# Five of eight pairs by seven products in the output projection, and the stream of weight sums at seven steps

## The chip, the core and the metric

The kernel runs on one core of a Trainium2 chip. The metric is the device time of one execution in microseconds, as the median of several runs. A core has a matrix engine (TensorE, PE in the profile, with PEld for its weight loads), a vector engine (VectorE, DVE), a scalar engine (ScalarE, ACT), GpSimd (POOL) and SyncE (SP), which here issues the loads. Each works through a queue of instructions of its own, in the order of that queue.

## The reference

One layer of a transformer block for 256 tokens and a model width of 2048, all in float32. Three attentions and a gate over them are followed by an output projection, and that by a feed-forward part with a causal convolution of three taps:

```python
merged = (g[:, :, 0] * (o_fox @ w_br_fox[l])
          + g[:, :, 1] * (o_sb @ w_br_sb[l])
          + g[:, :, 2] * (o_mem @ w_br_mem[l]))
x = x + merged @ w_out[l]                                  # 2048 x 2048

h2 = rms_norm(x, g_ffn[l])
u = causal_depthwise_conv(h2 @ w_up[l], conv_w[l], conv_b[l])   # 2048 x 11264
u_gate, u_val = jnp.split(u, 2, axis=-1)
x = x + (jax.nn.silu(u_gate) * u_val) @ w_down[l]          # 5632 x 2048
```

The change touches the last three matrix products.

## The kernel before

**Splits.** A float32 product is put together from rounded parts. Every piece of weights of 128 rows by 1024 columns is loaded into a `raw` buffer; ACT casts it to `hi` (L142 or L322) and DVE subtracts that from the raw piece to get `lo` (L143 or L323). `hi` and `lo` have four buffers each (`SBUFS`). The activations are split in the same way. In the output and down stages, a product of a weight block and an activation block is three matmuls (`three`, L328 to L330): `hi` with the high part, `hi` with the rest, and `lo` with the high part.

**Stages.** The queries, keys and values, the attentions and the gated branches come first. Then follow the output stage `o` (`w_out`, two blocks of 1024 output columns), the up stage `u` (`w_up`), and the down stage `d` (`w_down`, two blocks of 1024 columns, `nb` 0 and 1).

**Blocks.** `blocked` computes one such block. It walks over the pairs of 128-row tiles of the contraction (8 in `o`, 22 in `d`), and a plan string names what it does in turn. "e" is `eight`: the 2 x 2 block product of a pair by eight products, 24 matmuls. "s" is `seven`: the same by Strassen's seven products, 21 matmuls. For that, four sums T1 to T4 of the pair's weights are needed, and sums of its activations. "f" is `form`: the sums of the activations of the next pair, by `pair_sums` (8 instructions on DVE and some on ACT). Products that belong to several output blocks go to four extra banks Y, and `gather` adds these to the result `xres` on DVE behind the block's last seven, mixed with what follows it in the plan.

**Sums of weights.** For `o` and `d` the sums T1 to T4 are made in earlier stages, when DVE and the DMA queues have time: a pair of weight tiles is loaded into `pre_...`, `sums_in` makes the sums with three additions on DVE (L249 to L251), and the result is stored in DRAM as `kept_...`, from which `seven` reads them back. In the up stage the generator `pair_sums_ahead` does so, for all pairs of `d` that are left: it handles one pair in each `period` of steps, adds after `add` steps and stores after `store` steps. A step is one piece of the up stage. In the stages of the gates `seven_here` does without a store: it makes the sums with four additions of 512 columns in tiles of their own (`prepared`).

**Up stage.** 11 groups of 512 columns, `f0` from 0 to 40 in steps of four tiles, each in two halves (`s` 0 for the gate, 1 for the value). A half has 8 pieces; a piece is named by group, half and first tile, as in `lo_u_0_4` (the answers here leave out the group's number). Each piece has 8 matmuls of 512 columns with `hi` (L1231) and 8 of 256 with `lo` (L1232). Behind each half the convolution runs on ACT and DVE: `cr` (L1168), `u` (L1177), two filter steps `y` (L1183, L1184), the product `y` (L1190) and the split into `aT` (L177), on tiles of 256 columns.

**Order.** A scheduler of the framework sorts the instructions of each engine's queue, except those that are wrapped in `in_order` (`tc.keep_in_program_order`), which keep the order of the program among themselves. `later` puts a generator on a list of side work that `tick` advances by one step per piece.

Of the kernel before, what the change touches and what calls it, by code (L numbers as in the profile page):

```python
# [9 lines left out]
F32 = mybir.dt.float32  # L10
F32R = mybir.dt.float32r
# [31 lines left out]
def hybrid_block(  # L43
# [54 lines left out]
    def later(gen):  # L98
        waiting.append(gen)
# [24 lines left out]
    def finish():  # L124
        while waiting or active:
            tick(beside=False)
# [76 lines left out]
    def k_tiles(name):  # L203
# [19 lines left out]

    o_plans = ("eessesse", "eessesse")
    g_plans = (("", "esesesee", "esesesee"), ("esesesee", "esesesee", "esesesee"))
    d_plans = (
        "efefefef" + "sef" * 4 + "ssefsfssfssee",
        "efefef" + "sss" + "esss" * 3 + "ssee",  # L230
    )
    T1, T3, T4, T2 = range(4)
# [13 lines left out]

# [120 lines left out]
    def blocked(name, w, nb, n0, plan, pair, sums, raw_tile, t4_tile, gathered, ready=None, form=None, apart=None):  # L367
# [4 lines left out]
        ns = plan.count("s")  # L372

        def a_of(p, j, t):
            v = pair(p, j)
# [13 lines left out]
        def eight(p, first, last):  # L389
            by_bank = last and apart is not None  # L390
            w = []
            for j in range(2):
                w.append(parts(load(2 * p + j), f"{name}{nb}_{2 * p + j}"))
                if not by_bank:
                    for t in range(NT):
                        for n in range(2):
                            three(X[t][n], *a_of(p, j, t), w[j][n], first and j == 0, last and j == 1)
                go_on()
            if by_bank:
                for t in range(NT):  # L400
# [58 lines left out]
            three(Y[1], *f_of(p, FS2), T2w, first, last)  # L459
            go_on()  # L460

        by_seven = seven_here if name == "g" else seven
        ahead = {}
        s, e = 0, ns
        for i, c in enumerate(plan):
            if c == "s":
# [4 lines left out]
                by_seven(s, s == 0, s == ns - 1)  # L471
                s += 1
                if s == ns:
                    later(gathered(n0, Y))
            elif c == "f":
                form()
            else:
                eight(e, i == 0, i == len(plan) - 1)
                e += 1
            if name == "g" and plan[i + 1 : i + 2] == "s":  # L480
                ahead[s] = prepared(s)
        finish()
        return X

# [124 lines left out]
    def block(name, dt=F32):  # L609
        return bp.tile([P, 1024], dt, tag="blk", name=name)  # L610
# [384 lines left out]

    def merged_sums():
        yield 1
        for p in range(o_plans[0].count("s")):
# [119 lines left out]

    raw_o = lambda name: raw_tile(name, lambda name: gp.tile([P, PIECE], F32, tag="pre", bufs=1, name=name))
    t4_o = (junk, lambda name: block(name)[:, :512])  # L1120
    for nb, plan in enumerate(o_plans):
# [94 lines left out]
    for f0 in range(0, FT, 4):  # L1216
        if f0 == FA:
            assert not halves
            for g in background:
                deque(g, 0)  # L1220
            background.clear()
        for s in range(2):
            ps = [bank(f"u{f0 + i}_{s}") for i in range(4)]
            c0 = s * D_FF + f0 * P
            for k in range(0, KT, 2):
                hi, lo = piece(upv[:, k : k + 2, c0 : c0 + 512], 2, 512, f"u{f0}_{s}_{k}")
                for j in range(2):
                    first, last = k + j == 0, k + j == KT - 1
                    for i in range(4):
                        c = slice(i * P, (i + 1) * P)  # L1230
                        nc.tensor.matmul(ps[i], lhsT=hi[:, j, c], rhs=hT(k + j), start=first, stop=False)  # L1231
                        nc.tensor.matmul(  # L1232
                            ps[i][:, :S], lhsT=lo[:, j, c], rhs=hT(k + j)[:, :S], start=False, stop=last
                        )
# [16 lines left out]
        return dn[0].tile(shape, dt, tag=tag, name=name)  # L1251

    ov = out[0].rearrange("(t p) d -> p t d", p=P)
    N0, N1 = (plan.count("s") for plan in d_plans)
    sf = xt_pool.tile([P, 28, 2, P], F32R, tag="xt", name="sf")
    sf_more, sf_rest = [], []
    assert N0 == 11
# [3 lines left out]
    def s_of(p, f):  # L1261


        if f == FS1:
            return a_blocks[:, 2 * p, :, 1]
        if p < 9:
            return sf[:, 3 * p + f]
        if p == 9:
            return sf_more[0][:, f] if f < 2 else sf_rest[2]
        if p == 10:  # L1270
            return sf[:, 27] if f == 0 else sf_rest[f - 1]
        return a_blocks[:, 2 * (p - N0 + N1) + f // 2, :, f % 2]

    tmp_d = lambda name: place([P, PIECE], F32, "ts", name)

# [66 lines left out]
```

## Time and profile before

| | us |
|---|---|
| median of three runs | 1462.11 (1461.22 to 1462.31) |
| profiled execution | 1461.49 |
| its span on the core | 1459.8 |
| output stage, about | 658 to 743 |
| up stage, about | 743 to 1233 |
| down stage, first block, about | 1233 to 1345 |
| down stage, second block, about | 1345 to 1456 |

Times in the trace count from the start of the span. A row of the timeline gives the start, the duration, the engine, the line of the kernel, the operation, and what is written and read, with the number of equal instructions in a row; in brackets stands how long the engine was idle before it, and what released it. A row of the waits gives the waiting engine and its group, what released it, and then the sum, the number and the longest of those waits. In a table by windows the columns are busy times of PE, PEld, DVE, ACT and POOL, the granted clock, the share of the DMA engines and GB/s.

### The profile page before, as it was taken

To read this page: it belongs to the slowest core of one execution; us is meant where nothing else is said; L and a number is where in the kernel's file an instruction comes from. 1 tells how busy PE (TensorE), PEld (TensorE's weight loads), DVE (VectorE), ACT (ScalarE), POOL (GpSimd) and SP (SyncE) were. 2 spreads that over 40 slices of the span, in tenths; PEclk is the share of its full clock that TensorE was granted. 3 is DMA by queue.
4 is the path that set the end of the run, shared out by engine and by line. 5 is a ranking of instruction groups with operands and counts; after the bars stand their busy time and mean duration, and the time that the engine had idled before them with its cause. 6 is when DMAs were issued, how large, how long until landed. Compare 5 with 4: busy or idle time off the path is not lost.

```text
span 1459.8 us, 20547 instructions
## 1 busy us (share of the span) xinstructions
PE 1454.0 (100%) x7314; PEld 1230.1 (84%) x7314; DVE 1213.4 (83%) x1791; ACT 850.0 (58%) x1212; POOL 19.3 (1%) x48
## 2 busy tenths in 40 slices
PE   9999999999999999999999999999999999999998
PEld 7888888888888888888888888888888888888887
DVE  5778777776898899997887888888888877999878
ACT  6755454564564555545666556556556565676665
POOL 0000000010000000000000000000000000000000
PEclk9999999999999999999999999999999999999999
DMA  9697798777668576788877888888888866899995
GB/s 312 202 330 248 267 341 288 238 241 222 209 207 269 172 231 198 270 265 263 276 196 232 288 266 306 278 273 299 283 281 298 267 200 202 253 291 333 299 324 222
DMA packets 162534, 381.08 MB, mean 261 GB/s; under 512 B 12234, under 2 KB 27486, under 8 KB 158334
## 3 DMA queue, kind: packets, MB, share of 16 engines
q1 hardware_dynamic: 161022, 377.52, 78.9%
q10 hardware_dynamic: 1328, 2.11, 0.4%
q8 instruction: 57, 0.93, 0.3%
q14 instruction: 47, 0.39, 0.1%
q0 software_dynamic: 80, 0.13, 0.0%
HBM read 343.01 MB, written 36.70 MB: 260 GB/s over the span
## 4 chain that ended last, share of the span: by engine, by line
PE 97%; DVE 1%; DMA 1%; issue 0%; SPq 0%; ACT 0%; DVEq 0%; ACTq 0%
PE u L1231 22%; PE u L1232 11%; PE xd L329 3%; PE xd L330 3%; PE xd L328 3%; PE xg L330 3%; PE xg L329 3%; PE xg L328 3%; PE s L328 2%; PE s L330 2%; PE f L330 2%; PE f L328 2%; PE f L329 2%; PE s L329 2%; PE b L330 2%; PE b L328 2%
## 5 line engine op out<-in xcount | busy, mean ns | idle before, releaser
L1231 PE MATMUL u<-hT,hi_u 128*128 128x512 f32 x1232 | 428.3, 394 | 0.0
L1232 PE MATMUL u<-hT,lo_u 128*128 128x256 f32 x1232 | 341.3, 277 | 0.0
L1231 PEld LDWEIGHTS u<-hT,hi_u 128*128 128x128 f32 x1232 | 231.0, 188 | 53.8
L143 DVE TENSOR_TENSOR lo_u<-raw_u,hi_u 128x1024 fp32r<-128x1024 f32 x176 | 215.1, 1222 | 73.2 <-ACT hi_u L142 71.9
L142 ACT CAST hi_u<-raw_u 128x1024 fp32r<-128x1024 f32 x176 | 184.7, 1050 | 135.0 <-PE u L1231 106.7
L1232 PEld LDWEIGHTS u<-hT,lo_u 128*128 128x128 f32 x1232 | 231.2, 188 | 0.0
L323 DVE TENSOR_TENSOR lo_d<-raw_d,hi_d 128x1024 fp32r<-128x1024 f32 x88 | 106.7, 1222 | 16.2 <-ACT hi_d L322 13.8
L322 ACT CAST hi_d<-raw_d 128x1024 fp32r<-128x1024 f32 x88 | 91.7, 1053 | 38.8 <-PE xd L329 17.8
L322 ACT CAST hi_g<-raw_g 128x1024 fp32r<-128x1024 f32 (+1 forms) x80 | 77.1, 972 | 48.9 <-PE xg L329 19.2
L323 DVE TENSOR_TENSOR lo_g<-raw_g,hi_g 128x1024 fp32r<-128x1024 f32 (+1 forms) x80 | 88.6, 1119 | 4.1 <-ACT hi_g L322 4.1
L142 ACT CAST hi_f<-raw_f 128x1024 fp32r<-128x1024 f32 (+1 forms) x40 | 38.5, 967 | 51.8 <-PE f L329 42.8
L330 PE MATMUL xg<-lo_g,xT 128*128 128x512 f32 x175 | 68.1, 389 | 0.0
L329 PE MATMUL xg<-hi_g,xT 128*128 128x512 f32 x175 | 68.1, 389 | 0.0
L328 PE MATMUL xg<-hi_g,xT 128*128 128x512 f32 x175 | 68.1, 389 | 0.0
L143 DVE TENSOR_TENSOR lo_f<-raw_f,hi_f 128x1024 fp32r<-128x1024 f32 (+1 forms) x40 | 44.6, 1118 | 22.3 <-ACT hi_f L142 21.7
L143 DVE TENSOR_TENSOR lo_s<-raw_s,hi_s 128x1024 fp32r<-128x1024 f32 (+1 forms) x40 | 44.7, 1117 | 20.9 <-ACT hi_s L142 20.9
L1231 PE MATMUL u<-hT_rest,hi_u 128*128 128x512 f32 x176 | 62.0, 394 | 0.0
L142 ACT CAST hi_b<-raw_b 128x1024 fp32r<-128x1024 f32 x32 | 33.6, 1051 | 45.2 <-DMA raw_b<-in_w_br_fox_dram 15.8
L142 ACT CAST hi_s<-raw_s 128x1024 fp32r<-128x1024 f32 (+1 forms) x40 | 38.4, 961 | 36.8 <-PE s L329 23.9
L1182 ACT ACTIVATE y<-u,taps 128x256 f32<-128x256 f32 x88 | 49.6, 596 | 16.3 <-DVE u L1177 16.2
L330 PE MATMUL xd<-lo_d,aT 128*128 128x512 f32 x148 | 57.6, 389 | 0.0
L328 PE MATMUL xd<-hi_d,aT 128*128 128x512 f32 x148 | 57.6, 389 | 0.0
(520 smaller groups left out, 3473.1 us busy)
## 6 DMA issues: line engine op xcount, KB each, us to landing
raw_u<-in_w_up_dram SPq DMA_DIRECT2D x176, 512.0 KB, 4.5
raw_g<-in_w_in_dram SPq DMA_DIRECT2D x96, 512.0 KB, 4.4
raw_d<-in_w_down_dram SPq DMA_DIRECT2D x63, 512.0 KB, 5.4
pre_d<-in_w_down_dram SPq DMA_DIRECT2D x17, 1024.0 KB, 6.2
kept_d<-pre_d SPq DMA_DIRECT2D x17, 1024.0 KB, 6.2
raw_f<-in_w_in_dram SPq DMA_DIRECT2D x32, 512.0 KB, 4.9
raw_s<-in_w_in_dram SPq DMA_DIRECT2D x32, 512.0 KB, 5.2
raw_t_d<-kept_d SPq DMA_DIRECT2D x25, 512.0 KB, 5.8
```

What stands on the lines that cost most here:

```text
L142: pin(nc.scalar.copy(hi[:, :m], raw[:, :m]))
L143: pin(nc.vector.tensor_tensor(lo[:, :m], raw[:, :m], hi[:, :m].bitcast(F32), ALU.subtract))
L322: nc.scalar.copy(hi[:, :n], src)
L323: nc.vector.tensor_tensor(lo[:, :n], src, hi[:, :n].bitcast(F32), ALU.subtract)
L328: fix(nc.tensor.matmul(o, lhsT=ah, rhs=w[0], start=first, stop=False))
L329: fix(nc.tensor.matmul(o, lhsT=al, rhs=w[0], start=False, stop=False))
L330: fix(nc.tensor.matmul(o, lhsT=ah, rhs=w[1], start=False, stop=last))
L1182: nc.scalar.activation(y, u[:, 2:], AF.Identity, scale=tap(2), bias=tap(3))
L1231: nc.tensor.matmul(ps[i], lhsT=hi[:, j, c], rhs=hT(k + j), start=first, stop=False)
L1232: nc.tensor.matmul(ps[i][:, :S], lhsT=lo[:, j, c], rhs=hT(k + j)[:, :S], start=False, stop=last)
```

## The change

Each of the two output blocks does five of its eight pairs by seven, instead of three: pairs 0, 1, 2, 3 and 6 (`o_sevens`). The sums of the activations of pair 6 are made by a new generator `last_merged_sums` beside the first output block.

The stream of sums in the up stage makes one pair in 7 steps instead of 8, adds at once instead of after one step, and stores after 4 steps instead of 5. As the output stage takes four more pairs of those that are made early, this stream has 19 pairs to make instead of 17.

The second down block does 16 of its 22 pairs by seven instead of 14. For two of them, "i" in the plan, the sums are made on the spot: `begun` loads both tiles and makes three additions, and `seven_over` makes the fourth, both overwriting parts of the raw pieces. The plan's order is new: behind the last seven one "e" is left instead of two, and five "f" stand in it instead of three. The matmuls of the up stage are wrapped in `in_order`; they stand in the same order as before.

```diff
-    o_plans = ("eessesse", "eessesse")
+    o_plans = ("eessssse", "eessssse")
...
-        "efefef" + "sss" + "esss" * 3 + "ssee",
+        "efss" * 4 + "issefssisse",
...
+    o_sevens = (0, 1, 2, 3, 6)
+    pairs = lambda name, n: o_sevens if name == "o" else range(n)
...
-        for pr in range(plan.count("s"))
+        for pr, c in zip(pairs(name, 16), sevens(plan))
+        if c == "s"
...
+        def begun(p):
+            raw0, raw1, t13 = load(2 * p), load(2 * p + 1), tmp_d(f"t_{name}{nb}_{2 * p}")
+            b0, b1, u = (w.rearrange("p (n c) -> p n c", n=2) for w in (raw0, raw1, t13))
+            nc.vector.tensor_tensor(u[:, 0], b0[:, 0], b0[:, 1], ALU.add)
+            nc.vector.tensor_tensor(u[:, 1], b0[:, 1], b1[:, 1], ALU.add)
+            nc.vector.tensor_tensor(b0[:, 1], u[:, 0], b1[:, 1], ALU.add)
+            return raw0, raw1, t13
+
+        def seven_over(p, first, last):
+            raw0, raw1, t13 = ahead.pop(p)
+            (B00,) = parts(raw0[:, :512], f"{name}{nb}_{2 * p}")
+            three(Y[0], *a_of(p, 0, 0), B00, first, last)
+            nc.vector.tensor_tensor(raw0[:, :512], raw0[:, 512:], raw1[:, :512], ALU.add)
+            B10, B11 = parts(raw1, f"{name}{nb}_{2 * p + 1}")
...
+            T1w, T3w = parts(t13, f"t_{name}{nb}_{2 * p}")
...
+            T4w, T2w = parts(raw0, f"t_{name}{nb}_{2 * p + 1}")
...
+    def last_merged_sums():
+        yield 2
+        after = op.tile([P, KT, 2 * S], F32R, tag="ot", name="m_after")
+        ms[6] = after[:, 0:2].rearrange("p k c -> p (k c)").rearrange("p (f l q) -> p f l q", f=4, l=2)
+        pair_sums(mT[6], block("mw_6"), [(ms[6], slice(0, 4))])
...
-        pair_sums_ahead(lambda name: ends_tile(name, F32).rearrange("p i c -> p (i c)"), 8, 1, 5, delay=DU)
+        pair_sums_ahead(lambda name: ends_tile(name, F32).rearrange("p i c -> p (i c)"), 7, 0, 4, delay=DU)
...
-                        nc.tensor.matmul(ps[i], lhsT=hi[:, j, c], rhs=hT(k + j), start=first, stop=False)
...
+                        in_order(nc.tensor.matmul(ps[i], lhsT=hi[:, j, c], rhs=hT(k + j), start=first, stop=False))
```

DVE's queue in the up stage, group f0=12, first half, before the change, around the split of its third piece (`lo_u_0_4`):

```order
L251 TENSOR_TENSOR pre_d_0_8060<-pre_d_0_8060 128x512
L143 TENSOR_TENSOR lo_u_0_2_8137<-raw_u_0_2_8135,hi_u_0_2_8136 128x1024
L143 TENSOR_TENSOR lo_u_0_4_8181<-raw_u_0_4_8179,hi_u_0_4_8180 128x1024
L1168 TENSOR_TENSOR cr_1_8113<-cr_1_8113,u_1_7864 128x256
L1168 TENSOR_TENSOR cr_1_8124<-cr_1_8124,u_1_7865 128x256
L1177 TENSOR_TENSOR u_6990<-cr_1_8113,rbc 128x256
L1177 TENSOR_TENSOR u_6992<-cr_1_8124,rbc 128x256
L143 TENSOR_TENSOR lo_u_0_6_8203<-raw_u_0_6_8201,hi_u_0_6_8202 128x1024
L1183 TENSOR_SCALAR y_1_8117<-u_6990,taps,y_1_8117 128x256
L1183 TENSOR_SCALAR y_1_8128<-u_6992,taps,y_1_8128 128x256
```

The same place after the change (the lines of the code behind the new functions have larger numbers):

```order
L143 TENSOR_TENSOR lo_u_0_2_8166<-raw_u_0_2_8164,hi_u_0_2_8165 128x1024
L143 TENSOR_TENSOR lo_u_0_4_8210<-raw_u_0_4_8208,hi_u_0_4_8209 128x1024
L1208 TENSOR_TENSOR cr_1_8142<-cr_1_8142,u_1_7892 128x256
L1208 TENSOR_TENSOR cr_1_8153<-cr_1_8153,u_1_7893 128x256
L1217 TENSOR_TENSOR u_7018<-cr_1_8142,rbc 128x256
L1217 TENSOR_TENSOR u_7020<-cr_1_8153,rbc 128x256
L253 TENSOR_TENSOR pre_d_10_8231<-pre_d_10_8231 128x1024
L1223 TENSOR_SCALAR y_1_8146<-u_7018,taps,y_1_8146 128x256
L1223 TENSOR_SCALAR y_1_8157<-u_7020,taps,y_1_8157 128x256
L1224 TENSOR_SCALAR y_1_8146<-u_7018,taps,y_1_8146 128x256
```

and 15 rows further, the end of the same stretch:

```order
L1230 TENSOR_TENSOR y_0_7963<-y_0_7963,y_1_8190 128x256
L1230 TENSOR_TENSOR y_0_7972<-y_0_7972,y_1_8201 128x256
L255 TENSOR_TENSOR pre_d_10_8231<-pre_d_10_8231 128x512
L177 TENSOR_TENSOR aT<-y_0_7963,aT 128x256
L177 TENSOR_TENSOR aT<-y_0_7972,aT 128x256
L143 TENSOR_TENSOR lo_u_0_6_8238<-raw_u_0_6_8236,hi_u_0_6_8237 128x1024
L143 TENSOR_TENSOR lo_u_0_8_8260<-raw_u_0_8_8258,hi_u_0_8_8259 128x1024
```

Before, four instructions of the convolution stand between `lo_u_0_4` and `lo_u_0_6`, and the three additions of the stream's pair lie ahead, around the half's first pieces. After, 27 instructions stand there: 24 of the convolution and the three additions of `pre_d_10`.

DVE's queue at the program's end, before, from the addition of the second bank Y into `e`:

```order
L356 TENSOR_TENSOR e_13735<-e_13735,yd_1_12938 128x512
L323 TENSOR_TENSOR lo_d_42_13732<-raw_d_42_13729,hi_d_42_13731 128x1024
L323 TENSOR_TENSOR lo_d_43_13742<-raw_d_43_13739,hi_d_43_13741 128x1024
L358 TENSOR_TENSOR e_13735<-e_13735,yd_2_12939 128x512
L359 TENSOR_TENSOR xres_again<-xres_again,e_13735 128x512
L361 TENSOR_TENSOR e_13735<-e_13735,yd_3_12940 128x512
L362 TENSOR_TENSOR xres_again<-xres_again,e_13735 128x512
L364 TENSOR_TENSOR e_13735<-e_13735,yd_2_12939 128x512
L365 TENSOR_TENSOR xres_again<-xres_again,e_13735 128x512
L1303 TENSOR_TENSOR xres_again<-xres_again,xd_0_0_12786 128x512
```

After, from the last eight's first `lo`:

```order
L327 TENSOR_TENSOR lo_d_42_13820<-raw_d_42_13817,hi_d_42_13819 128x1024
L327 TENSOR_TENSOR lo_d_43_13826<-raw_d_43_13823,hi_d_43_13825 128x1024
L360 TENSOR_TENSOR e_13860<-e_13860,yd_1_12882 128x512
L362 TENSOR_TENSOR e_13860<-e_13860,yd_2_12883 128x512
L1346 TENSOR_TENSOR xres_again<-xres_again,xd_0_0_12828 128x512
L363 TENSOR_TENSOR xres_again<-xres_again,e_13860 128x512
L365 TENSOR_TENSOR e_13860<-e_13860,yd_3_12884 128x512
L1346 TENSOR_TENSOR xres_again<-xres_again,xd_0_1_12829 128x512
```

`lo_d_42` and `lo_d_43` are the pieces of the last eight. Before, all additions of `gather` stand ahead of those of that eight's banks (`xd`), and one eight more lies between them and the last bank Y; after, the two kinds alternate.

More of the change, by code (lines that the diff above doesn't have):

```diff
@@ L229, in hybrid_block @@
         "efefefef" + "sef" * 4 + "ssefsfssfssee",
-        "efefef" + "sss" + "esss" * 3 + "ssee",
+        "efss" * 4 + "issefssisse",
     )
+    sevens = lambda plan: [c for c in plan if c in "si"]
     T1, T3, T4, T2 = range(4)
@@ L371, in blocked @@
         Y = []
-        ns = plan.count("s")
+        ns = len(sevens(plan))
         def a_of(p, j, t):
@@ L460, in seven_here @@
             go_on()
-        by_seven = seven_here if name == "g" else seven
+        def begun(p):
[11 more added lines that the diff above has]
+            B10, B11 = parts(raw1, f"{name}{nb}_{2 * p + 1}")
+            three(X[0][0], *a_of(p, 1, 0), B10)
+            three(X[0][1], *f_of(p, FS4), B11)
+            go_on()
+            T1w, T3w = parts(t13, f"t_{name}{nb}_{2 * p}")
+            three(Y[2], *f_of(p, FS1), T1w, first, last)
+            three(Y[3], *f_of(p, FS3), T3w, first, last)
+            T4w, T2w = parts(raw0, f"t_{name}{nb}_{2 * p + 1}")
+            three(X[1][0], *a_of(p, 1, 1), T4w)
+            three(Y[1], *f_of(p, FS2), T2w, first, last)
+            go_on()
+        by_seven = {"s": seven_here if name == "g" else seven, "i": seven_over}
         ahead = {}
-        s, e = 0, ns
+        s, e = 0, 0
+        sp = pairs(name, ns)
+        ep = [p for p in range(len(plan) - plan.count("f")) if p not in sp]
         for i, c in enumerate(plan):
-            if c == "s":
+            if c in "si":
                 if s == 0:
@@ L477, in blocked @@
             else:
-                eight(e, i == 0, i == len(plan) - 1)
+                eight(ep[e], i == 0, i == len(plan) - 1)
                 e += 1
@@ L481, in blocked @@
                 ahead[s] = prepared(s)
+            elif plan[i + 1 : i + 2] == "i":
+                ahead[s] = begun(s)
         finish()
@@ L997, in merged_sums @@
         yield 1
-        for p in range(o_plans[0].count("s")):
+        for p in range(4):
             ms[p] = block(f"ms_{p}", F32R).rearrange("p (f l q) -> p f l q", f=4, l=2)
@@ L1120, in hybrid_block @@
     t4_o = (junk, lambda name: block(name)[:, :512])
+    later(last_merged_sums())
     for nb, plan in enumerate(o_plans):
@@ L1230, in hybrid_block @@
                         c = slice(i * P, (i + 1) * P)
-                        nc.tensor.matmul(ps[i], lhsT=hi[:, j, c], rhs=hT(k + j), start=first, stop=False)
-                        nc.tensor.matmul(
-                            ps[i][:, :S], lhsT=lo[:, j, c], rhs=hT(k + j)[:, :S], start=False, stop=last
+                        in_order(nc.tensor.matmul(ps[i], lhsT=hi[:, j, c], rhs=hT(k + j), start=first, stop=False))
+                        in_order(
+                            nc.tensor.matmul(
+                                ps[i][:, :S], lhsT=lo[:, j, c], rhs=hT(k + j)[:, :S], start=False, stop=last
+                            )
                         )
@@ L1253, in hybrid_block @@
     ov = out[0].rearrange("(t p) d -> p t d", p=P)
-    N0, N1 = (plan.count("s") for plan in d_plans)
+    N0, N1 = (len(sevens(plan)) for plan in d_plans)
     sf = xt_pool.tile([P, 28, 2, P], F32R, tag="xt", name="sf")
@@ L1271, in s_of @@
             return sf[:, 27] if f == 0 else sf_rest[f - 1]
-        return a_blocks[:, 2 * (p - N0 + N1) + f // 2, :, f % 2]
+        over = a_pair(p - N0 + N1).rearrange("p k (l t q) -> p k l t q", l=2, t=NT)
+        return over[:, f // 2, :, f % 2]
     tmp_d = lambda name: place([P, PIECE], F32, "ts", name)
```

2 lines of the change are left out of this document (1 added, 1 removed).

## The prediction

> **What bounds the kernel now.** I read the page's first two parts, then TensorE's waits, its steps in the timeline, and then the chain of work behind it in the up stage and in the last down block.
>
> ```profile
> span 1459.8 us, 20547 instructions
> PE 1454.0 (100%) x7314; PEld 1230.1 (84%) x7314; DVE 1213.4 (83%) x1791; ACT 850.0 (58%) x1212; POOL 19.3 (1%) x48
> PEclk9999999999999999999999999999999999999999
> PE spare L92 <- DVE qscale L531: 1.2, 1, 1.2
> PE kv L154 <- DVE memT L185: 0.5, 2, 0.2
> ```
>
> TensorE is busy for the whole span at its full granted clock, and the only waits of PE that the waits view lists are three at the very start, 1.7 us together. So the time is the count of matmuls times their step. Whatever another engine does is free until it makes TensorE wait once; from then on it counts in full. The change therefore has two sides: matmuls it removes, and waits it creates on an engine that has none.
>
> The step of a matmul is not its record, since they overlap:
>
> ```profile
> 1299.81 0.39 PE L328 MATMUL xd<-hi_t_d,aT 128*128 128x512 f32 x1
> ...
> 1311.83 0.39 PE L330 MATMUL yd<-lo_d,sf 128*128 128x512 f32 x1
> ```
>
> 53 steps of the down stage lie between these two starts, 12.02 us, so 0.227 us each.
>
> The work that feeds TensorE in the up stage is the split of every 128x1024 piece of weights into `hi` (a cast on ACT) and `lo` (a subtraction on DVE):
>
> ```profile
> L1231 PE MATMUL u<-hT,hi_u x1232: 389/395/474, 743.2 to 1230.0; 128*128 128x512 f32 x176
> L1232 PE MATMUL u<-hT_rest,lo_u x176: 274/277/280, 764.7 to 1233.0; 128*128 128x256 f32 x176
> ACT hi_u L142 <- PE u L1231: 106.7, 92, 1.9
> 917.07 1.05 ACT L142 CAST hi_u<-raw_u 128x1024 fp32r<-128x1024 f32 x1 [1.67 <-PE u L1231]
> 918.15 1.23 DVE L143 TENSOR_TENSOR lo_u<-raw_u,hi_u 128x1024 fp32r<-128x1024 f32 x1 [0.68 <-ACT hi_u L142]
> ```
>
> From 743.2 to 1233.0 are 490 us for 22 half groups of 8 pieces, 176 pieces: 2.78 us a piece. The casts waited 92 times, 106.7 us, for TensorE to give a `hi` buffer back: there are four, so the stock of split pieces is full most of the time, and it cannot be larger. How much time that stock is follows from the last two rows. TensorE ended a piece at about 917.07, and the buffer's next piece is wanted three pieces later, 917.07 + 3 x 2.78 = 925.4. Its `lo` is ready at 918.15 + 1.23 = 919.38. The lead is 6.0 us. It is the number on which this forecast turns: if DVE does other work W between two `lo_u`, the second one is ready W + 1.14 after the first, and is wanted 2.78 after it. So TensorE waits when W + 1.14 is over 6.0 + 2.78, that is W over **7.6 us**.
>
> Before, the trace has a drawdown of that kind without harm, at the stage's start:
>
> ```profile
> 768.43 1.23 DVE L143 TENSOR_TENSOR lo_u<-raw_u,hi_u 128x1024 fp32r<-128x1024 f32 x1 [0.53 <-ACT hi_u L142]
> 775.48 2.36 DVE L143 TENSOR_TENSOR lo_u<-raw_u,hi_u 128x1024 fp32r<-128x1024 f32 x2 [5.49 <-ACT hi_u L142]
> ```
>
> The two starts are 7.05 us apart, under the 8.8 us that the stock bears, and PE does not wait. There ACT and not DVE was late; it is the longest that the up stage shows.
>
> **Matmuls removed.** A pair by eight takes 24 matmuls and one by seven 21. Each o block turns one pair, the second down block two: 4 x 3 = 12 matmuls, 12 x 0.227 = **-2.7 us**. That is all that TensorE can win, and it is 0.19%. About 0.2%, 2.9 us, is what a measurement of this kernel tells from no change.
>
> **The o stage.** Two more sevens read stored sums, and the activations' sums of pair 6 are made beside the first block; DVE has free time there, and the streams that feed it come from earlier stages. I cost it at nothing. If the cover is gone, a late load costs up to a load's spare time, under 1 us each.
>
> **The up stage.** Its stream makes 19 pairs of sums instead of 17, one in 7 steps instead of 8. The price of two more is small in sum. What counts is where their three additions lie in DVE's queue:
>
> ```profile
> 923.70 1.23 DVE L143 TENSOR_TENSOR lo_u<-raw_u,hi_u 128x1024 fp32r<-128x1024 f32 x1 [0.16 <-ACT hi_u L142]
> 924.84 0.87 DVE L1183 SCALAR_TENSOR_TENSOR y<-u,taps,y 128x256 f32<-128x256 f32 x2
> 925.64 0.88 DVE L1184 SCALAR_TENSOR_TENSOR y<-u,taps,y 128x256 f32<-128x256 f32 x2
> 926.43 0.75 DVE L1190 TENSOR_TENSOR y<-y,y 128x256 f32<-128x256 f32 x2
> 927.10 0.41 DVE L1168 TENSOR_TENSOR cr<-cr,u 128x256 f32<-128x256 f32 x1
> 927.43 0.75 DVE L177 TENSOR_TENSOR aT<-y,aT 128x256 fp32r<-128x256 f32 x2
> 936.51 1.22 DVE L249 TENSOR_TENSOR pre_d<-pre_d 128x1024 f32<-128x1024 f32 x1
> 937.64 0.42 DVE L177 TENSOR_TENSOR aT<-y,aT 128x256 fp32r<-128x256 f32 x1
> 937.98 0.69 DVE L250 TENSOR_TENSOR pre_d<-pre_d 128x512 f32<-128x512 f32 x1
> 938.58 1.22 DVE L143 TENSOR_TENSOR lo_u<-raw_u,hi_u 128x1024 fp32r<-128x1024 f32 x1
> 939.71 0.69 DVE L251 TENSOR_TENSOR pre_d<-pre_d 128x512 f32<-128x512 f32 x1
> 940.38 1.23 DVE L143 TENSOR_TENSOR lo_u<-raw_u,hi_u 128x1024 fp32r<-128x1024 f32 x1
> ```
>
> From start to start: an addition of 256 columns 0.33 (927.10 to 927.43), a step of the filter 0.40 (two from 924.84 to 925.64), an addition of the stream 1.13 for the wide one and 0.60 and 0.67 for the others, a `lo` 1.14. Before, the stream's additions and the filter's stand between the `lo_u` in small lots. In the changed order the period of 7 walks through the 16 pieces of a group, and in four places the additions fall into one lot with the filter, with no `lo_u` between. The worst, shown with the change, is in group f0=12 from `lo_u_0_4` to `lo_u_0_6`: 16 additions of 256 columns, 8 filter steps, 3 additions of the stream, 5.3 + 3.2 + 2.4 = 10.9 us. Counted in the same way the other three lots are 8.9 (21 instructions, ending at a `lo_u_0_8`), 8.1 (19, `lo_u_1_6`) and 8.4 us (20, `lo_u_0_4`). Two more of 5.3 us follow a piece that is already late, and just pass.
>
> Over the 7.6 us that the stock bears, these are 3.3 + 1.3 + 0.5 + 0.8 = 5.9 us of waits of TensorE. With a lead 0.15 us larger, about what is left uncertain in reading it, 5.3. That is the lower end, since DVE cannot leave the order of its queue. The upper end counts whole records (0.42, 0.48, 1.22, 0.69) instead of starts: about 0.085 us more for each of these 87 instructions, 7.4 us, 13.3 together. The truth lies near the lower end, since the rows show the starts, but something comes on top: filter steps and `aT` lean on ACT, which does a 1.05 us cast between them, and in a lot they wait for it one after the other. I allow 0.4 us for each of the four, and take **+7.5 us** (5.3 to 13.3).
>
> [...]
>
> The matmuls of `u` (L1231, L1232) are now kept in program order; they stand in the same order before, so this costs nothing. The loads of the stream raise SyncE's traffic by two pairs in 490 us, which is hidden by the same stock.
>
> **The second down block.** Two pairs by seven have their sums made on the spot, and two more activation sums are formed within the block.
>
> ```profile
> 1344.00:1400.00 56.00, 56.00 (x248) 46.37 (x248) 47.45 (x64) 35.22 (x46) 0.00 (x0) 1.00 0.91 297
> 1400.00:1456.00 56.00, 55.83 (x252) 46.25 (x250) 46.34 (x49) 33.23 (x36) 0.00 (x0) 1.00 0.77 275
> L323 DVE TENSOR_TENSOR lo_d<-raw_d,hi_d 128x1024 fp32r<-128x1024 f32 x42 | 51.0, 1223 | 8.5 <-ACT hi_d L322 6.5
> L337 DVE TENSOR_TENSOR fw<-aT 128x512 f32<-128x512 f32 x3 | 2.1, 687 | 0.0
> L346 DVE TENSOR_TENSOR aT<-fw,aT 128x128 fp32r<-128x128 f32 x12 | 2.7, 286 | 0.0
> raw_d<-in_w_down_dram SPq DMA_DIRECT2D x23, 512.0 KB, 6.1
> ```
>
> DVE (fourth column of times) is busy 47.45 and 46.34 us in these 56 us each: 18.2 us are free. A pair on the spot needs 3.5 `lo`, 4.0 us, and four additions of 512 columns, 2.5 us, against two `lo`, 2.3 us: 4.2 more, 8.4 for both. A form is an addition of 0.7 us (L337), four of 0.22 (L346, 2.7 us for 12) and three small ones between them, about 2.5 us, two of them 5.0. So 13.4 of the 18.2 us are used up: in sum it just fits, with little to spare. The two raw pieces of such a pair are held until its last sums are split, so the loads behind them start late, and a load takes 6.1 us; I put that at 0 to 1 us.
>
> The end is worse placed. Of the two pairs by eight that stood behind the last seven one is left:
>
> ```profile
> 1443.81 0.39 PE L330 MATMUL yd<-lo_t_d,aT 128*128 128x512 f32 x1
> 1444.95 0.68 DVE L356 TENSOR_TENSOR e<-e,yd 128x512 f32<-128x512 f32 x1
> ...
> 1455.55 0.28 PE L330 MATMUL apart<-lo_d,a_ends 128*128 128x256 f32 x1
> 1455.95 0.42 DVE L1307 TENSOR_TENSOR xres_again<-xres_again,apart 128x256 f32<-128x256 f32 x1
> 1456.40 0.34 ACTq L1308 DMA_DIRECT2D out_dram<-xres_again  x1
> ```
>
> From TensorE's last matmul into Y1 to its last of all were 11.74 us. With one eight (24 x 0.227 = 5.4) less, 6.3 are left, and behind that Y1 and the last `lo` DVE still has 11 additions of 512 columns, at about 0.66 us 7.3 us, and one of 0.42. It ends 1.1 us later than TensorE lets it before. That is the floor; with the late loads and DVE's own backlog up to 4. I take **+2.5 us**.
>
> **Sum.** 1461.49 (the profiled execution) - 2.7 + 7.5 + 2.5 = 1468.8. The median of the runs is 0.62 above the profiled one: **1469.4 us**.
>
> **Rivals.**
> *The lots do no harm* (the lead is longer than I read, or ACT and DVE catch up): it decides at a lead of 9.3 us, five pieces and more. Against it stand the four buffers and the 92 waits for one of them. Then -2.7 + 1.1 to 4 at the end: 1460.5 to 1463.4, no measurable change. 0.14.
> *All is hidden*, the end too, and only the matmuls count: 1459.4; faster by over 0.2% only with the measurement's spread. 0.03.
> *The lots are stretched by ACT and the loads*: DVE's queue waits in each lot for a cast or an addition's 1 MB load, as at 775.48, where 5.49 us went. With 2 to 3 us for each of the four, 8 to 12 more than my 1.6: 1476 to 1480. 0.13.
> *TensorE slows down after waits.* The trace has one such stretch:
>
> ```profile
> 1.23 2.42 PE L92 MATMUL spare<-idle 128*128 128x384 bf16 x7 [1.23 <-DVE qscale L531]
> 6.39 0.39 PE L153 MATMUL kv<-hi_kv,memT 128*128 128x512 f32 x1
> 6.62 0.40 PE L154 MATMUL kv<-hi_kv,memT 128*128 128x512 f32 x1
> ```
>
> At the start seven matmuls of 384 columns take 2.42 us, 0.35 each, though by the later step of 0.23 for 512 they would take 0.17: half pace, for some 4 us, though the granted clock of the page shows 9 there too. If a wait of 3.3 us or more does that again, each costs about 2 us, one to three of them: 1471 to 1476. 0.12. [...]
>
> **Chances.** The forecast's own case (1466 to 1473) 0.58. The range that leaves out 2 in 10, part of the first rival and the far end of the third, is 1463.0 to 1478.5. Faster 0.03, same (1459.2 to 1465.0) 0.14, slower 0.83.
>
> **What would show it.** In the changed trace TensorE's waits should list `u` waiting for DVE's `lo_u`, four to six times, the longest about 3 to 4 us near the `lo_u_0_6` of f0=12, and the gaps before it filled with DVE rows and no `lo_u`. Behind the last matmul DVE should run for 1 to 3 us more. If the page shows PE without waits in the up stage, the lead is wrong and the first rival holds; if waits sit in the o stage or in the middle of the second down block, I have placed the price wrongly.

## The result, and the profile after

The changed kernel takes **1483.72 us** (median of five runs, 1478.64 to 1487.17) against 1461.61 (1461.22 to 1462.31): a ratio of **1.0147** (95% interval 1.0126 to 1.0168), 22 us slower. The forecast was 1469.4 with a range to 1478.5. The direction was right and the size was not. Two numbers of the text ahead of the prediction are wrong: before the change each output block did four of its eight pairs by seven, not three, and the two blocks together now take two more stored pairs, not four. This is why the stream makes 19 pairs instead of 17, and the prediction's 12 matmuls are counted rightly.

The page's head, of the profiled execution, which took 1487.17 us and is the slowest of the five:

```profile
span 1485.5 us, 20646 instructions
PE 1468.0 (99%) x7302; PEld 1235.7 (83%) x7302; DVE 1233.9 (83%) x1834; ACT 858.8 (58%) x1229; POOL 19.1 (1%) x48
```

TensorE has its 12 matmuls less, and is busy 14.0 us longer all the same. So a list of waits cannot hold the whole loss. Of the waits of PE:

```profile
PE u L1273 <- DVE lo_u L143: 7.5, 4, 4.4
PE yd L334 <- DVE lo_d L327: 2.0, 2, 1.2
...
PE hT L196 <- DVE xres_again L1169: 0.5, 1, 0.5
PE xd L334 <- DVE lo_d L327: 0.2, 1, 0.2
```

The four waits of `u` for `lo_u` are there, 7.5 us in all. What else became longer is seen when starts are compared. A half group has 8 pieces of 16 matmuls. From one start to the start 128 matmuls later, in the middle of the up stage, before:

```profile
999.84 0.40 PE L1231 MATMUL u<-hT,hi_u 128*128 128x512 f32 x1
...
1022.02 0.40 PE L1231 MATMUL u<-hT,hi_u 128*128 128x512 f32 x1
```

and after:

```profile
1004.66 0.40 PE L1271 MATMUL u<-hT,hi_u 128*128 128x512 f32 x1
...
1027.27 0.40 PE L1271 MATMUL u<-hT,hi_u 128*128 128x512 f32 x1
```

22.18 us before, 22.61 after: 2.77 and 2.83 us a piece, with nothing waited for between, and a granted clock of 1.00 in both. In the changed kernel's trace 172 of the 172 pieces counted (the first three are left out, and the few with a wait in them count by the pattern around them) run at 2.83; before, none does. That is about 0.053 x 172 = 9.1 us which no view of waits shows. The step is long from the first counted piece, at 755.0 us, and the first of the four waits comes 136 us later: in this execution the waits did not bring it about.

The longest wait, in DVE's timeline of after:

```profile
880.59 1.22 DVE L143 TENSOR_TENSOR lo_u<-raw_u,hi_u 128x1024 fp32r<-128x1024 f32 x1 [0.58 <-ACT hi_u L142]
...
883.50 1.22 DVE L253 TENSOR_TENSOR pre_d<-pre_d 128x1024 f32<-128x1024 f32 x1 [0.26 <-DMA pre_d<-in_w_down_dram]
...
890.67 0.98 DVE L1223 SCALAR_TENSOR_TENSOR y<-u,taps,y 128x256 f32<-128x256 f32 x2 [0.78 <-ACT y L1222]
...
893.03 0.68 DVE L255 TENSOR_TENSOR pre_d<-pre_d 128x512 f32<-128x512 f32 x1
...
894.30 3.49 DVE L143 TENSOR_TENSOR lo_u<-raw_u,hi_u 128x1024 fp32r<-128x1024 f32 x3
```

From one `lo_u` to the next are 13.7 us: 1.2 for the `lo` itself, 10.9 by the sum of starts for the lot of 27 instructions that the changed order shows, and the rest, 1.6, in or around waits for the stream's load and for ACT (0.26 and 0.78 in the rows above, 0.22 in one not shown). The granted clock (last but two) around it:

```profile
885.00:890.00 5.00, 5.00 (x30) 4.34 (x29) 4.67 (x13) 3.63 (x5) 0.00 (x0) 1.00 0.48 181
890.00:895.00 5.00, 1.12 (x7) 0.71 (x5) 4.32 (x10) 2.81 (x6) 0.00 (x0) 0.94 0.12 49
895.00:900.00 5.00, 4.43 (x14) 3.85 (x15) 3.92 (x4) 0.00 (x0) 0.00 (x0) 0.50 0.96 333
900.00:905.00 5.00, 5.00 (x26) 4.30 (x26) 1.40 (x2) 2.10 (x2) 0.00 (x0) 0.88 1.01 374
```

TensorE stands still for 4.4 us and then runs at half clock: 14 matmuls in five microseconds instead of 30. Over the two pieces concerned this is 2.8 us on top of the wait.

The same lot stops the loads. The stream's store (L292 before, L296 after) stands in SyncE's queue ahead of the pieces' loads, and waits for the last of the three additions. Before, and after:

```profile
SPq L292 <- DVE pre_d L251: 2.3, 15, 0.2
```

```profile
SPq L296 <- DVE pre_d L255: 26.4, 13, 7.9
```

The end, of after:

```profile
1479.95 0.28 PE L334 MATMUL apart<-lo_d,a_ends 128*128 128x256 f32 x1
1482.18 0.42 DVE L1350 TENSOR_TENSOR xres_again<-xres_again,apart 128x256 f32<-128x256 f32 x1
```

DVE's last addition begins 2.2 us behind the last matmul's start; before it was 0.4.

By stages, the 25.7 us between the two spans are: up to the head of the up stage 1.6 (TensorE's first products began and ran later by 2.0 in this execution, ahead of all that the change touches; nothing of it is put down to the change), the up stage 20.3, the second and first down block 2.5 (with six matmuls, 1.4 us, less), what lies behind the last matmul 1.3. The up stage's 20.3 are the waits (7.5), the half clock (2.8), the longer step (9.1), and nearly 1 more. Most of that is what a wait costs beyond its listed length. It is listed from the end of one record to the next start, but without a wait the records overlap. The pieces with the other three waits, of 1.38, 0.25 and 1.39 us, took 1.64, 0.51 and 1.65 us longer than 2.83: 0.26 more each.

### The profile page after: what moved, and what is told of

The parts are those of the page before. It is cut to its first block, busy times and chain, and to the rows that moved or that the text cites. A ratio compares the mean times of both kernels' runs of the same rounds, so it can differ in the third digit from the quotient of the medians.

```text
span 1485.5 us, 20646 instructions
## 1 busy us (share of the span) xinstructions
PE 1468.0 (99%) x7302; PEld 1235.7 (83%) x7302; DVE 1233.9 (83%) x1834; ACT 858.8 (58%) x1229; POOL 19.1 (1%) x48
## 4 chain that ended last, share of the span: by engine, by line
PE 93%; DVE 3%; DMA 3%; issue 0%; ACT 0%; SPq 0%; DVEq 0%; ACTq 0%
PE u L1271 20%; PE u L1273 10%; PE xg L334 4%; PE xg L333 4%; PE xg L332 4%; PE xd L334 3%; PE xd L333 3%; PE xd L332 3%; PE s L332 2%; PE s L334 2%; PE f L334 2%; PE f L332 2%; PE f L333 2%; PE s L333 2%; PE b L332 2%; PE b L333 2%
## 5 line engine op out<-in xcount | busy, mean ns | idle before, releaser
L1271 PE MATMUL u<-hT,hi_u 128*128 128x512 f32 x1232 | 438.9, 400 | 0.0
L1273 PE MATMUL u<-hT,lo_u 128*128 128x256 f32 x1232 | 347.7, 282 | 7.5 <-DVE lo_u L143 7.5
L326 ACT CAST hi_d<-raw_d 128x1024 fp32r<-128x1024 f32 (+1 forms) x88 | 90.7, 1043 | 41.0 <-PE xd L333 12.1
L327 DVE TENSOR_TENSOR lo_d<-raw_d,hi_d 128x1024 fp32r<-128x1024 f32 (+1 forms) x88 | 105.0, 1207 | 9.2 <-ACT hi_d L326 7.8
L332 PE MATMUL s<-hi_s,xT 128*128 128x512 f32 (+1 forms) x140 | 54.1, 386 | 0.0
L326 ACT CAST hi_t_g<-t_g 128x1024 fp32r<-128x1024 f32 x30 | 31.5, 1051 | 38.2 <-PE xg L333 36.6
```

The costliest lines, as they stand in the source:

```text
L326: nc.scalar.copy(hi[:, :n], src)
L327: nc.vector.tensor_tensor(lo[:, :n], src, hi[:, :n].bitcast(F32), ALU.subtract)
L332: fix(nc.tensor.matmul(o, lhsT=ah, rhs=w[0], start=first, stop=False))
L1271: in_order(nc.tensor.matmul(ps[i], lhsT=hi[:, j, c], rhs=hT(k + j), start=first, stop=False))
L1273: nc.tensor.matmul(ps[i][:, :S], lhsT=lo[:, j, c], rhs=hT(k + j)[:, :S], start=False, stop=last)
```

## The experiments

Three theories at the start. *Lots*: TensorE's waits come from where the stream's additions stand in DVE's queue, and half clock follows the long ones. *Step*: the longer step is a second pattern into which TensorE falls by chance of a few ns. Against it, that the pin or the additional traffic causes it. *End*: the rest is the single eight behind the last seven, and the sums on the spot. Medians stand beside those of the kernel before on the same chip.

**The stream.**

e12, the stream's numbers alone, in the kernel before:

```diff
-pair_sums_ahead(..., 8, 1, 5, delay=DU)
+pair_sums_ahead(..., 7, 0, 4, delay=DU)
```

> The kernel before with its stream at 7, 0, 4 and nothing else changed (17 pairs, plans as before). By the order of DVE's queue three of the four lots are there, 3.2, 1.2 and 0.3 us over the bound. Theory of the lots: waits of TensorE for lo_u of 5 to 8 us in all, the longest 3 to 4.5 us in group f0=12, a stretch at half clock behind it, and 0 to 9 us by the step's pattern: 1468 to 1480. Rival, that the two additional pairs or the other plans are needed for the loss: under 2 us more than before, 1461 to 1464.

1473.65 us against 1461.45, ratio 1.0077 (1.0064 to 1.0090).

```profile
PE u L1232 <- DVE lo_u L143: 4.4, 4, 2.8
```

This one line, with no pair more, no pin and no plan changed, brings the waits (4.4 us, a little under the 4.7 that three of this order's lots have over the bound of 7.6 us and under the 5 to 8 expected), 3.4 us at half clock, and the longer step in 77 of 172 pieces, 12 us in all. The rival is out.

e1, the changed kernel with the old numbers, begun earlier so that 19 pairs fit:

```diff
-pair_sums_ahead(..., 7, 0, 4, delay=DU)
+pair_sums_ahead(..., 8, 1, 5, delay=7)
```

> The changed kernel, but the up stage's stream of sums at the old 8 steps a pair (adding after 1, storing after 5), begun 15 steps earlier so that its 19 pairs still fit. By the order of DVE's queue no lot of work between two lo_u is longer than 4 us then. Theory of the lots: the four waits of TensorE for lo_u (7.5 us) and the stretch at half clock behind the longest (about 2.7 us) go, so about 10 us less than the changed kernel's 1483.7, 1472 to 1475, with no wait of u for lo_u. Theory of the step: what is left of the up stage's loss is a step of TensorE of 2.83 us a piece instead of 2.77 (9.2 us over 176 pieces). If the lots or the gaps cause that step too, it goes as well and the time is 1464 to 1466.

1466.80 against 1462.14, ratio 1.0044 (1.0025 to 1.0062): 17 us of the 22 are gone. In its trace PE has no listed wait for `lo_u`, 171 of 172 pieces run at 2.77 us, and the clock stays at 1.00. What is left is about as much as the plan of the second down block costs alone (e10, below). Three of the ten runs took 1473.5 to 1474.7, though. No profile was taken of those.

e6, the changed kernel's period of 7 with the old offsets:

```diff
-pair_sums_ahead(..., 7, 0, 4, delay=DU)
+pair_sums_ahead(..., 7, 1, 5, delay=DU)
```

> The changed kernel with its stream at 7 steps, but adding after one step and storing after five, as before the change. By the order of DVE's queue, two lots are left over the 7.6 us bound, from the same walk that gave 3.2, 1.2, 0.3 and 0.6 us for the changed kernel: 1.2 us at a lo_u_0_8 in group f0=12 and 1.2 us at a lo_u_0_6 in group f0=28. Theory of the lots: TensorE waits for lo_u at these two places, 1 to 2.5 us each, nowhere for over 3 us, and no stretch at half clock follows. Time 1467 to 1478, by which of its two patterns the step falls into. Rival, that the stream's speed and not its place in the queue makes the waits: waits as in the changed kernel, 7.5 us, longest over 4 us.

1485.61 against 1462.44, ratio 1.0159 (1.0145 to 1.0173). A miss: slower than any.

```profile
PE u L1273 <- DVE lo_u L143: 9.5, 5, 3.6
SPq L305 <- DMA kept_d<-pre_d: 36.5, 16, 5.5
DVE pre_d L253 <- DMA pre_d<-in_w_down_dram: 4.0, 2, 2.5
```

The two lots are there, but the waits at them are 1.8 and 3.6 us, and there are three more, one of 3.1. Two stretches at half clock followed (a granted clock of 0.50 from 935 to 941, and 0.62 over 1081 to 1084). The lots of the order were not all. Storing after 5 of 7 steps leaves two steps, 5.5 us, to the next load, and both use the same tile. The load's issue waited for the store in SyncE's queue (36.5 us in 16 times, up to 5.5), so it came late, and DVE's addition, which stands ahead of a lot and of the next `lo_u`, waited for it up to 2.5 us. This stands ahead of the wait of 3.1 us. The longest, 3.6 at 1081.4, has no such load ahead of it: there DVE had waited 2.4 us for a copy on ACT, which waited for TensorE, and two lots followed each other. A sum over DVE's queue that takes every operand as ready sees neither. In the changed kernel, with three steps between, DVE's wait for the load was 0.3 us at the most.

**The step.**

e2, the kernel before with the pin alone (`in_order` around the two matmuls of the up stage).

> The kernel before, with nothing changed but the up stage's matmuls kept in program order. Theory that the pin slows TensorE's step: 2.83 us a piece, 1461.6 + 9.2 = 1471. Theory that the two additional pairs of sums (loads, stores, additions) slow it: nothing changes, 1461.6. Theory that the step falls into one of two patterns by chance of a few ns at the stage's start: either of the two, 1461.6 or 1471, but nothing between.

1461.53 against 1462.14, ratio 0.9998 (0.9989 to 1.0007); all 172 pieces at 2.77. In the kernel before, the pin costs nothing.

e3, the changed kernel without the pin.

> The changed kernel without the pin on the up stage's matmuls. By the order of DVE's queue the lots stay, three of the four (the fourth, 0.6 us, goes). Theory that the pin slows TensorE's step: 2.77 us a piece, 9.2 us less, about 1474, with waits of 7 us left. Theory that the additional sums slow it: 2.83 us, 1482 to 1484. Chance: either.

1478.50 against 1462.14, ratio 1.0106 (1.0085 to 1.0128). 73 pieces at 2.83 and 99 at 2.77, in turns. Neither of the two theories that ask for one step throughout holds. The waits for `lo_u` missed too: 7 us were expected, and 3.2 in two waits are listed, the longest 2.7. With the stream at 7, 0, 4, the three traces with the pin (the changed kernel, e4, e9) list 7.1 to 7.5 us (longest 3.8 to 4.4), the two without it (e3, e12) 3.2 and 4.4 (2.7 and 2.8). The pin also puts DVE's and ACT's instructions in another order at a few places. Whether it makes the waits longer was not settled, as the profiled execution here was the fastest of four.

e5, the kernel before with a small matmul at the head of 20 half groups:

```diff
+if k + j == 0 and f0 > 0:
+    m = 64 + 8 * (f0 // 2 + s)
+    nc.tensor.matmul(ps[0][:, :m], lhsT=hi[:, 0, :P], rhs=hT(0)[:, :m], start=True, stop=True)
```

> The kernel before, with one small additional matmul (64 to 232 columns, into a bank that the next matmul overwrites) at the head of each of the up stage's half groups but the first two, 20 in all. In themselves they cost about 0.1 to 0.2 us each, 2 to 4 us together. Theory that TensorE's step has two patterns that hold from one disturbance to the next: half groups of 2.77 us a piece and of 2.83 us a piece both occur, changing only at the head of a half group, with no wait of TensorE and no other change in load; the time rises by the 2 to 4 us and 0.43 us for each half group in the slow pattern, 1464 to 1474. Rival, that the slow step comes from the changed kernel's additional sums or from the load on the memory: all pieces at 2.77 us, 1464 to 1466.

1469.44 against 1462.44, ratio 1.0051 (1.0037 to 1.0064). The first matmul behind the added one, in three half groups in a row and the next:

```profile
879.51 0.45 PE L1234 MATMUL u<-hT,hi_u 128*128 128x512 f32 x1
...
901.82 0.44 PE L1234 MATMUL u<-hT,hi_u 128*128 128x512 f32 x1
...
924.12 0.44 PE L1234 MATMUL u<-hT,hi_u 128*128 128x512 f32 x1
...
946.84 0.45 PE L1234 MATMUL u<-hT,hi_u 128*128 128x512 f32 x1
```

22.31, 22.30 and 22.72 us, with about 0.06 us of added matmul in each: two of them in the short pattern, one in the long. Of the 20 half groups 13 run in the long one, 7 in the short one, and the change from one to the other comes only at an added matmul. TensorE waits for nothing in the up stage of this trace, and neither the loads nor the sums differ from before. 13 x 0.42 us and 20 added matmuls of 0.04 to 0.10 (from start to start) are 6.9 of the 7.0 us. So the same instructions have two paces, and a disturbance of tens of ns picks one until the next.

e9, the changed kernel once more, one run.

> The changed kernel once more, unaltered. Theory that TensorE's step falls into one of two patterns by a few ns at each disturbance: the waits for lo_u are the same four, 7 to 8 us, but the pieces in the slow pattern need not be the same ones; the time lies in 1476 to 1487 according to how many there are. Rival, that this program's step is slow of itself: 2.83 us in all pieces again.

1479.97 us.

```profile
PE u L1273 <- DVE lo_u L143: 7.1, 4, 3.8
```

The waits are the same four, 0.4 us less in sum; but now 104 pieces run long and 68 short, where the first profile had 172 long. It starts short, as e1, e3 and e6 did, turns long at the 38th piece, short again behind the wait in the 115th, and long at the 150th. At the 38th and the 150th DVE has a lot of 11 instructions, 5.3 us from start to start: the two that the prediction had "just pass". No wait of TensorE is listed there, so the list does not show what turned the pace. Chance in the pace would account for the spread of the program's runs, 1478.64 to 1487.17, when those of before lie within 1.1 us; this is argued, as only two of its executions have a profile.

**The second down block and the output stage.**

e4, the changed kernel with the old plan of the second down block.

> The changed kernel with the old plan of the second down block (14 pairs by seven, none on the spot, two eights at the end); the output stage and the up stage as changed. All theories: the up stage as in the changed kernel, waits of 7.5 us and 2.83 us a piece unless chance has it otherwise. The second down block loses its waits for lo_d (2.2 us) and the later end behind the last matmul (1.3 us), and gets 6 matmuls back (1.4 us): about 2 us less than the changed kernel, 1481 to 1482.

1476.05 against 1462.14, ratio 1.0087 (1.0068 to 1.0107). 7.5 us of waits for `lo_u`, 101 long pieces. The difference from the changed kernel mixes the block's gain with the step's chance, so e10 is the cleaner run.

e10, the new plan of that block alone, with output plans and stream as before (four pairs by seven in each output block, no `last_merged_sums`):

```diff
-o_plans = ("eessssse", "eessssse")
+o_plans = ("eessesse", "eessesse")
...
-pair_sums_ahead(..., 7, 0, 4, delay=DU)
+pair_sums_ahead(..., 8, 1, 5, delay=DU)
```

> The new plan of the second down block alone: output plans as before, the stream at 8, 1, 5 with its old start (17 pairs), matmuls of the up stage pinned. Theory: no wait in the up stage, all its pieces from the third on at 2.77 us; in the second down block six matmuls less (1.4 us), waits for lo_d of 1.5 to 2.2 us, and DVE's end about 1.9 us later behind the last matmul: 2 to 3 us more than before, 1464 to 1465. Rival, that these waits come from traffic or a backlog that the changed output and up stages leave behind: no more than 1 us of them here, 1462 to 1463.

1465.76 against 1461.45, ratio 1.0031 (1.0020 to 1.0041): 4.3 us slower with six matmuls less. All 172 pieces of the up stage are short. What the waits and the end show:

```profile
DVE t_d L469 <- DMA raw_d<-in_w_down_dram: 4.7, 2, 2.9
PE yd L334 <- DVE lo_d L327: 1.5, 2, 0.8
```

```profile
1457.94 0.28 PE L334 MATMUL apart<-lo_d,a_ends 128*128 128x256 f32 x1
...
1460.47 0.42 DVE L1349 TENSOR_TENSOR xres_again<-xres_again,apart 128x256 f32<-128x256 f32 x1
```

The first addition of a pair on the spot stands in DVE's queue ahead of the `lo_d` of the pieces now due. Its raw piece was loaded too late, DVE waited for it twice, up to 2.9 us, and TensorE behind it.

```profile
1400.89 0.39 PE L333 MATMUL yd<-hi_d,aT 128*128 128x512 f32 x1
1402.08 0.50 PE L334 MATMUL yd<-lo_d,aT 128*128 128x512 f32 x1 [0.80 <-DVE lo_d L327]
1402.42 0.39 PE L332 MATMUL yd<-hi_d,sf 128*128 128x512 f32 x1
```

The wait of 0.80 us costs about 1.1: the two steps take 1.53 us, where two without a wait take 0.45. By such starts, six places of this block lose 3.4 us, where the list of waits has 1.7. And the last addition begins 2.5 us behind the last matmul's start, against 0.4 before.

e7, the changed output stage and the stream of e1, with the old plan of the second down block.

> The changed output stage with the stream at 8 steps begun 15 earlier, and the old plan of the second down block. Theory: no lots, no late end, six matmuls fewer than before (1.4 us). If nothing else is lost, 0.7 to 1.4 us faster than before, 1460.7 to 1461.4; a wait of hT behind the output stage (0.3 to 0.5 us in the runs so far) and a step in the slow pattern (up to 9 us) speak against it.

1462.39 against 1462.44, ratio 1.0006 (0.9992 to 1.0020). The gain that was expected, 0.7 to 1.4 us, does not show. The early stream is not free: the trace lists two waits for `lo_u` near its head, 1.1 us together.

e8, the same with 15 pairs by seven, one on the spot, and two eights at the end:

```diff
-"efss" * 4 + "issefssisse",
+"efss" * 4 + "sseissssee",
```

> As the run before, but the second down block does 15 pairs by seven, one of them on the spot, with two eights behind the last seven: plan efss four times, then sseissssee. Theory that the late end comes from the single eight behind the last seven: no late end, at most one wait of about 1 us behind the on-the-spot pair; nine matmuls fewer than before (2.0 us). 1460 to 1462. Rival, that sums on the spot cost their place wherever they stand (DVE's time and late loads): waits for lo_d of 1 us and more stay, 1462 to 1464.

1470.47 against 1462.44, ratio 1.0054 (1.0041 to 1.0066). No wait for `lo_d` is listed in its trace, though DVE waited 0.7 us for the raw piece, and the last addition begins 0.4 us behind the last matmul's start, as before the change. So the late end comes with the single eight, and a sum on the spot can be free. But one wait of 2.0 us for `lo_u` near the head of the stream that begins early threw the step into the long pattern for 151 pieces, and that decides the time.

e11, the changed output stage with the old stream; the two pairs that it lacks are made on the spot early in the second down block, two eights at the end:

```diff
-"efss" * 4 + "issefssisse",
+"efefefsss" + "eiss" + "esis" + "esss" + "ssee",
...
-pair_sums_ahead(..., 7, 0, 4, delay=DU)
+pair_sums_ahead(..., 8, 1, 5, delay=DU)
```

> The changed output stage with the up stage's stream exactly as before (8, 1, 5, 17 pairs): the two pairs of sums that it lacks are made on the spot in the second down block, early (plan efefefsss eiss esis esss ssee, 14 pairs by seven, two eights at the end). Theory: no wait in the up stage, no late end, six matmuls fewer (1.4 us); the wait of hT behind the output stage up to 0.5, waits for lo_d up to 0.5 each. 1460.5 to 1462. Rival, that sums on the spot cost a wait of 1 us each wherever they stand: 1462.5 to 1463.5.

1461.23 against 1461.45, ratio 1.0002 (0.9989 to 1.0014). Its waits of PE are a single line, the one at the program's start:

```profile
PE spare L92 <- DVE qscale L564: 1.2, 1, 1.2
```

DVE waits for a raw piece here too (1.0 and 0.6 us), but TensorE does not wait behind it, and the last addition begins 0.4 us behind the last matmul's start. Nothing is lost, and six matmuls (1.4 us, 0.09%) are below what the runs can tell. One of its 12 runs took 1471.59, as two of e7's 11 took 1468.82 and 1469.61; no profile was taken of those, and that the long pattern is behind them, as behind the three of e1, is argued, not shown. No version beat the kernel before.

## Why the prediction was right or wrong

**The lots in DVE's queue**: right in mechanism and place. The prediction had four waits, 7.5 us, the longest 3 to 4 near the `lo_u_0_6` of f0=12; measured are four, 7.5 us, the longest 4.4 there. That the sums agree so closely is luck: with the 0.4 us allowed for each, the forecast was 3.7, 1.7, 0.9 and 1.2, and the list has 4.4, 1.4, 0.2 and 1.4, each costing about 0.26 more than listed. In the longest lot ACT and the stream's load took 1.6 us, not 0.4.

**The step of TensorE** is the term that failed. "From 743.2 to 1233.0 are 490 us ... 2.78 us a piece" was taken as a property of these instructions, and the sum had no term for it. It is one of two paces. The kernel before held the short one in its trace; the changed kernel ran in the long one through the whole up stage of its profiled execution and through part of it in another (e9). In the first, the other pace cost 9.1 us, which is half of the error there (1487.17 against the sum's 1468.8) and the part that no rival held. What picks the pace at the head of the stage stayed open: it was long there in two traces, the changed kernel's and e4's, and short in the twelve others. The sentence that the pinned order "costs nothing" was right for the kernel before (e2), and the longer step is not the pin's doing: e12 has it without the pin.

**Half clock after waits** was a rival with a chance of 0.12, "about 2 us" for each wait of 3.3 us or more. It happened once, for 2.8 us. It should have been part of the forecast itself, since the forecast's own longest wait already was at that length. No run shows 3.3 us as a limit: in e8 half clock came behind a wait of 2.0 us.

**The second down block** was sized at +2.5 us against 1.4 saved. e10 shows 4.3 net, so 5.7 without the saved matmuls. The floor for the end, 1.1, was too low: in the changed kernel DVE's last addition begins 1.8 us later behind the last matmul (2.2 against 0.4), of which 1.3 are left at the span's end. DVE began the 11 additions 1.2 us behind TensorE's last matmul into Y1, which the sum did not count in full. The loads of pairs on the spot, "0 to 1 us", cost more: about 3.4 us in e10. The prediction looked at the loads queued behind those pieces. The late one was their own, and the wait stood in DVE's queue ahead of work that was due.

**The output stage** "at nothing": right within 0.7 us. From the stage's first matmul to the up stage's first are 84.36 us before and 83.71 after: 0.65 less, where six matmuls are 1.36. Of the 0.7 lost, 0.5 is the one wait of `hT`.

**Rivals.** That the lots do no harm is refuted by e12 and e1. That ACT and the loads stretch each lot by 2 to 3 us did not happen in the changed kernel (1.6 us in the longest), but did in e6, where the store comes a step later and one lot waited 2.5 us for a load.

## What to carry to other kernels

Where one engine is busy without a gap, compare the pace of its instructions from start to start, and not only its waits: 9 of the 25.7 us of the profiled execution were lost without any. A listed wait is a lower bound of what it costs where records overlap: by 0.26 us in the up stage here, and 0.80 listed against about 1.1 in e10. Where a stream of side work has a period, look in the order of the queue for the places at which it meets the other side work, and weigh the longest lot against the time that the stock of buffers holds. An instruction that may wait for a load should stand ahead of work that is due only where the stock bears the wait.

## What the runs showed of the hardware

The same matmuls at the same granted clock of 1.00 have two paces, 2.77 and 2.83 us for 16 (the traces before and after). In e5 they kept the one they were in up to an added matmul, and one of 128 columns was enough: 22.30 us for the half group ahead of it, 22.72 for the one behind. Why there are two stayed open.

The length of a wait does not decide alone whether half clock follows. In e3 TensorE stood still for 2.7 us here and went on at full clock:

```profile
888.00:891.00 3.00, 0.32 (x2) 0.18 (x2) 3.00 (x7) 0.82 (x3) 0.00 (x0) 1.00 0.41 175
891.00:894.00 3.00, 3.00 (x19) 2.68 (x20) 3.00 (x3) 0.00 (x0) 0.00 (x0) 1.00 0.99 301
```

In e8 it stood still for 2.0 us, and the clock fell:

```profile
815.00:818.00 3.00, 0.96 (x6) 0.61 (x5) 3.00 (x5) 2.75 (x5) 0.00 (x0) 1.00 0.51 216
818.00:821.00 3.00, 3.00 (x12) 2.59 (x11) 3.00 (x7) 1.64 (x6) 0.00 (x0) 0.58 0.97 311
```

The prediction's rival asked for a wait of 3.3 us or more. The 4.4 us of the changed kernel agree with it; the 2.0 us of e8 do not. The granted clock behind these two and five other waits:

| run | the wait (us) | granted clock behind it |
|---|---|---|
| e8 | 2.0 | 0.58 over 818 to 821 |
| e3 | 2.7 | 1.00 over 891 to 894 |
| e12 | 2.8 | 0.50 over 892 to 895 |
| e6 | 3.1 | 0.50 over 935 to 938 |
| e6 | 3.6 | 0.62 over 1081 to 1084 |
| e4 | 4.1 | 0.50 over 893 to 896 |
| changed kernel | 4.4 | 0.50 over 895 to 900 |

The waits of e3 and e12 are hardly of different length, and the clock fell behind one of them only. What decides beside the length was not shown.
